# Norm scales applied to the results of the products instead of to the tokens, in a three-block model on one Trainium2 core

## The chip, the core and the metric

The kernel runs on one core of one Trainium2 chip. The core has TensorE (PE, matrix products; its weight loads are shown as PEld), VectorE (DVE), ScalarE (ACT), GpSimd (POOL), and SyncE (SP), which only issues DMAs here. The metric is the device time of one execution in microseconds (us); lower is better. A profile is one execution recorded by the hardware profiler, and its times are counted from its first instruction.

## The reference, cut to what matters

1024 tokens of width 1024 go through three blocks, each with RMS norms in front of its large products. All is float32.

```python
def rmsnorm(x, g):
    xf = x.astype(jnp.float32)
    y = xf * lax.rsqrt(jnp.mean(xf * xf, axis=-1, keepdims=True) + NORM_EPS)
    return (y * g.astype(jnp.float32)).astype(x.dtype)
# block 1
h = rmsnorm(x, norm_g[l]);  proj = h @ w_in[l]                # 1024 -> 4608, split into nine parts
kv = rmsnorm(mem, mem_norm_g[l]) @ w_mem_kv[l]                # 256 memory rows -> 1024
# mLSTM, differential attention, attention on the memory, gates silu(z)
x = rmsnorm(x + concat(y_m, y_d, y_c) @ w_out[l], final_g)
# block 2
proj = rmsnorm_2(h, norm_mix[l]) @ w_in[l]                    # attention, spatial gating, gates
h = h + merged @ w_out[l]
g, up = jnp.split(rmsnorm_2(h, norm_ffn[l]) @ w_ffn_in[l], 2, axis=-1)
h = rmsnorm_2(h + (jax.nn.silu(g) * up) @ w_ffn_out[l], norm_final)
# block 3
proj = rmsnorm_3(h, norm_mix_g[l]) @ w_in[l]                  # recurrent unit, gated convolution
h = h + y @ w_out[l]
m = rmsnorm_3(h, norm_mlp_g[l]) @ w_mlp_up[l]
h = h + jnp.square(jax.nn.relu(m)) @ w_mlp_down[l]
out = rmsnorm_3(h, norm_final_g)
```

At the two joints between blocks two norms are chained: the final norm of a block, whose result is also the next block's residual, and the first norm of the next block.

## The kernel before

**Layout.** Tokens lie transposed: a page `u[k]` has 128 features on the partitions and 1024 tokens along the row, and `h` = 0, 1 picks the half of 512 tokens. A scale per token is therefore a value per column, which must be spread over all partitions.

**Products.** A float32 product is made as three products of a high and a low part (`mm3`, L149 to L151). `split` (L158, L159) makes the parts: ScalarE rounds the source to the high part, VectorE subtracts it for the low part. Weights come in units of 512 KB over SP's queue and are split at L76 and L77. `gemm_fm` runs units of 8 x 3 products of 128x512 into one of two PSUM banks (`ps_mm`, two buffers), then calls `evict`, which reads the bank; TensorE can start unit n+2 only when the bank of unit n is read. With `lag` the first units run all their first halves before any second half.

**The order of the work.** The program is written as generators: a main one that issues product units, and side ones (`spawn`) that advance by one step at each `tick`, about one per unit. A scheduler then puts every engine's instructions in an order by priority (evictions have a raised one); on the chip each engine works its own list in order, so an instruction that waits holds up all behind it.

**A seam** (`seam`, then `norm_gen`, L405). The last output product of a stage (`gemm_out`, first half and then second half of the tokens) adds its results to the pages `u` (L692, L1252, L1646). ScalarE squares each result (L186, L189), GpSimd adds the squares up (L190; at a joint twice, since each of the two chained norms has its own sum). When a half is complete, TensorE sums over the partitions (L198), VectorE takes the inverse root in about a dozen small operations (L174 to L179, L420 to L423), TensorE spreads it over the partitions (L210), ScalarE copies it to SBUF (L433). Only then does VectorE multiply each page by gain and scale (L436), and `split` makes the parts that the next products read. The next `gemm_fm` waits for them.

**The start.** Memory and tokens are loaded; the memory's squares are summed (L186 to L190), its scale is made (L198, L565, L174 to L179, L210, L569), it is scaled (L574) and split, and only then do the eight units on the memory run (four in `gemm_fm`, four in `gemm_tm`). The tokens of each half are squared and added on ScalarE and VectorE (L549, L551), and pass `norm_gen`.

**Other places that are touched.** `block_gemm` (L311) makes two by two blocks of products with seven instead of eight multiplications: GpSimd forms sums of weights (L330 to L335), `operand` splits them, and `out` gets the four result blocks C11, C12, C21, C22 of each pair (L1313 to L1319 in block 2: a silu of C11 and C12; L1667, L1679, L1680 in block 3: a squared relu). `block_tokens` makes the token operands of it and overwrites `u`; `block_up` starts it when the norm generators are done. `residual` (L447) reloads a block's residual and multiplies it by the final norm's gain and scale (L457), the scale being read from DRAM. `down_loads` (L394) reloads hidden values. Evictions of `gemm_fm` write to SBUF with ScalarE's copy or activation, or with both engines.

Of the kernel before, what the change touches and what calls it, by code (L numbers as in the profile page):

```python
# [23 lines left out]
LEAD = dict(norm_g=1, norm_mix_2=3, norm_ffn_2=3, norm_mix_g_3=3, norm_mlp_g_3=3)  # L24
LEAD_F = 2
# [3 lines left out]
LAG = 3  # L29
# [66 lines left out]
class Kern:  # L96
# [56 lines left out]
    def split(self, dst, off, n, src, scale=None):  # L153

        nc = self.nc
        hi, lo = dst[:, 0, off:off + n], dst[:, 1, off:off + n]
        if scale is None:
            nc.scalar.copy(hi, src)  # L158
            nc.vector.tensor_sub(lo, src, hi.bitcast(F32))  # L159
        else:  # L160
            nc.scalar.activation(hi, src, AF.Copy, scale=scale)
            nc.vector.scalar_tensor_tensor(lo, src, scale, hi.bitcast(F32), op0=OP.mult, op1=OP.subtract)
# [50 lines left out]
    def gemm_fm(self, n_units, src, evict, halves=(0, 1), N=512, lag=1, gate=None, post=None, wait=None, ahead=True):  # L213
# [5 lines left out]
        for i, (u, h) in enumerate(order):  # L219
# [7 lines left out]
            for k in range(8):  # L227
# [177 lines left out]
    def norm_gen(self, h, u, g, xs, acc, acc2=None, fg=None, r_d=None, lead=1, stay=False):  # L405

        nc = self.nc  # L410
        n2 = 8 if fg is not None else 4
        for _ in range(lead):
            yield
        ps = self.tp()
        self.sums_to_cols(ps, 0, acc, 4)
        if fg is not None:
            self.sums_to_cols(ps, 4, acc2, 4)
        v = self.nsm.tile([128, 8], F32, name="nv")
        r = self.nsm.tile([128, 8], F32, name="nr")
        nc.vector.tensor_scalar(v[:, :4], ps[:, :4], 1.0 / 1024, EPS, op0=OP.mult, op1=OP.add)  # L420
        if fg is not None:
            nc.vector.tensor_scalar(v[:, 4:], ps[:, 4:8], 1.0 / 1024, None, op0=OP.mult)
            nc.vector.scalar_tensor_tensor(v[:, 4:], v[:, :4], EPS, v[:, 4:], op0=OP.mult, op1=OP.add)  # L423
        self.rsqrt(r[:, :n2], v[:, :n2], n2)
        if fg is not None:
            gg = self.nsm.tile([128, 8], F32, name="ngg")
            nc.vector.tensor_mul(gg, fg, g)
        else:
            gg = g
        yield  # L430
        bps = self.bcast_cols(r[:, n2 - 4:], 4)
        b1 = self.page((128, 2, 512), F32, "rbc")
        nc.scalar.copy(b1[:, 0, :], bps)  # L433
        for k in range(8):
            t = u(k, h) if stay else self.half_tmp("nt")
            nc.vector.scalar_tensor_tensor(t, u(k, h), gg[:, k:k + 1], b1[:, 0, :], op0=OP.mult, op1=OP.mult)  # L436
            x = self.split_page()
            xs[k, h] = x
            self.split(x, 0, 512, t)
            if k % 2:  # L440
                yield
        if fg is not None:
            bps = self.bcast_cols(r, 4)
            nc.scalar.copy(b1[:, 1, :], bps)
            nc.sync.dma_start(r_d[:, h * 512:h * 512 + 512], b1[:, 1, :])
            yield

    def residual(self, u, d, fg, page, name):

        nc = self.nc  # L450
        r = self.page(name="rres")
        nc.gpsimd.dma_start(r, d[8])
        for k in range(8):
            t = page(name=name)
            nc.gpsimd.dma_start(t, d[k])
            yield
            nc.vector.scalar_tensor_tensor(t, t, fg[:, k:k + 1], r, op0=OP.mult, op1=OP.mult)  # L457
            u.append(t)
# [62 lines left out]
    def block1(self):  # L521
# [11 lines left out]
        for i in range(2):  # L533
            (nc.sync if i else nc.scalar).dma_start(memx[i], A["memT"][i])
# [3 lines left out]
        for h in (0, 1):  # L538
            for k in range(8):
# [1188 lines left out]
    def final_gen(self, o, n, u3, acc):  # L1728
        nc, v = self.nc, self.v
        if o + n < 1024:  # L1730
            for _ in range(LEAD_F):
                yield
# [400 lines left out]
```

## Time and profile before

| | us |
|---|---|
| time, median of 3 runs | 3388.26 (3388.24 to 3388.63) |
| time of the profiled execution | 3385.71 |
| span of the profile, first to last instruction | 3383.9 |
| TensorE busy in the span | 3266.0 (97%) |
| VectorE, ScalarE, GpSimd busy | 1937.2, 1169.3, 510.2 |
| mean granted TensorE clock | 0.987 of full speed |

The span is the profiled execution without 1.8 us around it. A busy time counts the instructions' own durations; matrix products overlap, so a busy TensorE is not one at its peak. The granted clock is the share of full speed that the chip allowed TensorE; at the start of the trace, before 30.9 us, none is recorded and the views show 1.00 there.

### The profile page before, as it was taken

To read this page: it belongs to the slowest core of one execution; us is meant where nothing else is said; L and a number is where in the kernel's file an instruction comes from. 1 tells how busy PE (TensorE), PEld (TensorE's weight loads), DVE (VectorE), ACT (ScalarE), POOL (GpSimd) and SP (SyncE) were. 2 spreads that over 40 slices of the span, in tenths; PEclk is the share of its full clock that TensorE was granted. 3 is DMA by queue.
4 is the path that set the end of the run, shared out by engine and by line. 5 is a ranking of instruction groups with operands and counts; after the bars stand their busy time and mean duration, and the time that the engine had idled before them with its cause. 6 is when DMAs were issued, how large, how long until landed. Compare 5 with 4: busy or idle time off the path is not lost. (4 is left out here: it accounts for less than half of the span.)

```text
span 3383.9 us, 41750 instructions
## 1 busy us (share of the span) xinstructions
PE 3266.0 (97%) x16039; PEld 2666.3 (79%) x16039; DVE 1937.2 (57%) x3619; ACT 1169.3 (35%) x2115; POOL 510.2 (15%) x461
## 2 busy tenths in 40 slices
PE   6999999999999999999999999999999989999998
PEld 6788877677777888887788877878878778878887
DVE  7465566664755562446755566455569765554444
ACT  5222344433444442213433342134443433332211
POOL 0000000002200000102423220040211243220002
PEclk9999999999999999999999999999999999999999
DMA  5133211322211244422122244121112233362211
GB/s 188 58 103 127 87 57 38 113 69 78 72 46 42 70 147 159 143 94 103 66 84 85 81 179 148 57 97 54 46 51 75 103 103 109 112 251 94 69 50 56
DMA packets 128632, 318.52 MB, mean 94 GB/s; under 512 B 16305, under 2 KB 34865, under 8 KB 128433
## 3 DMA queue, kind: packets, MB, share of 16 engines
q1 hardware_dynamic: 104976, 236.63, 20.5%
q0 software_dynamic: 21440, 76.51, 6.4%
q8 instruction: 126, 2.06, 0.3%
q10 hardware_dynamic: 2016, 2.72, 0.2%
q14 instruction: 74, 0.60, 0.1%
HBM read 232.90 MB, written 82.90 MB: 93 GB/s over the span
## 5 line engine op out<-in xcount | busy, mean ns | idle before, releaser
L149 PE MATMUL mm<-sp,wsplit 128*128 128x512 f32 (+1 forms) x2880 | 1151.0, 400 | 30.0 <-ACT sp L158 9.7
L150 PE MATMUL mm<-sp,wsplit 128*128 128x512 f32 (+1 forms) x2880 | 1132.4, 393 | 9.5 <-DVE sp L159 7.1
L151 PE MATMUL mm<-sp,wsplit 128*128 128x512 f32 (+1 forms) x2880 | 1129.7, 392 | 0.0
L149 PEld LDWEIGHTS mm<-sp,wsplit 128*128 128x128 f32 x2880 | 547.1, 190 | 149.2 <-ACT sp L158 14.1
L150 PEld LDWEIGHTS mm<-sp,wsplit 128*128 128x128 f32 x2880 | 548.5, 190 | 117.3 <-DVE sp L159 10.2
L151 PEld LDWEIGHTS mm<-sp,wsplit 128*128 128x128 f32 x2880 | 547.7, 190 | 111.4 <-issue 0.4
L358 PE MATMUL mm<-sp,wsplit 128*128 128x512 f32 x1632 | 390.5, 391 | 6.6 <-ACT scp L362 5.0
L76 ACT CAST wsplit<-wraw 128x1024 fp32r<-128x1024 f32 x196 | 205.7, 1049 | 494.3 <-PE mm L151 468.3
L358 PEld LDWEIGHTS mm<-sp,wsplit 128*128 128x128 f32 x1632 | 306.5, 188 | 73.5 <-ACT scp L362 5.4
L77 DVE TENSOR_TENSOR wsplit<-wraw,wsplit 128x1024 fp32r<-128x1024 f32 x196 | 244.8, 1250 | 152.7 <-ACT wsplit L76 145.1
L358 PE MATMUL sc<-sp,wsplit 128*128 128x512 f32 x1224 | 296.6, 391 | 1.3 <-DVE c L372 1.3
L358 PEld LDWEIGHTS sc<-sp,wsplit 128*128 128x128 f32 x1224 | 231.1, 189 | 51.0 <-DVE c L372 1.7
L190 POOL TENSOR_TENSOR acc<-acc,sqt 128x512 f32<-128x512 f32 (+1 forms) x105 | 140.1, 1346 | 474.9 <-ACT sqt L189 388.3
L1646 DVE TENSOR_TENSOR ur<-ur,mm 128x512 f32<-128x512 f32 x112 | 76.8, 686 | 152.1 <-PE mm L151 152.1
L159 DVE TENSOR_TENSOR wsplit<-ssum,wsplit 128x512 fp32r<-128x512 f32 x136 | 101.8, 750 | 89.1 <-ACT wsplit L158 88.9
L1252 DVE SCALAR_TENSOR_TENSOR ur<-mm,ur 128x512 f32<-128x512 f32 x96 | 66.2, 689 | 106.5 <-PE mm L151 106.3
L158 ACT CAST wsplit<-ssum 128x512 fp32r<-128x512 f32 x136 | 82.9, 621 | 109.8 <-POOL ssum L335 36.0
L158 ACT CAST sp<-hraw 128x512 fp32r<-128x512 f32 x108 | 64.0, 620 | 65.2 <-PE mm L151 44.1
L333 POOL TENSOR_TENSOR ssum<-ssum,wraw 128x512 f32<-128x512 f32 x34 | 51.9, 1527 | 221.7 <-DVE wsplit L159 221.7
L158 ACT CAST wsplit<-wraw 128x512 fp32r<-128x512 f32 x102 | 61.8, 620 | 67.4 <-PE sc L358 47.8
L159 DVE TENSOR_TENSOR sp<-hraw,sp 128x512 fp32r<-128x512 f32 x108 | 71.3, 686 | 11.6 <-ACT sp L158 11.6
L335 POOL TENSOR_TENSOR ssum<-wraw,ssum 128x512 f32<-128x512 f32 x34 | 47.3, 1390 | 196.9 <-DVE wsplit L159 196.9
(550 smaller groups left out, 4234.2 us busy)
## 6 DMA issues: line engine op xcount, KB each, us to landing
wraw<-W SPq DMA_DIRECT2D x264, 512.0 KB, 3.7
hraw<-hid_d POOLq DMA_DIRECT2D x54, 512.0 KB, 6.0
hid_d<-scp SPq DMA_DIRECT2D x68, 256.0 KB, 2.0
t_d<-gl SPq DMA_DIRECT2D x32, 256.0 KB, 2.0
u<-x_d POOLq DMA_DIRECT2D x16, 512.0 KB, 6.0
gl<-t_d POOLq DMA_DIRECT2D x32, 256.0 KB, 3.1
u_d<-u SPq DMA_DIRECT2D x32, 256.0 KB, 2.0
ur<-u_d POOLq DMA_DIRECT2D x16, 512.0 KB, 8.2
```

The lines of the kernel that those rows point to most:

```text
L76: K.nc.scalar.copy(s[:, 0, :], r)
L77: K.nc.vector.tensor_sub(s[:, 1, :], r, s[:, 0, :].bitcast(F32))
L149: t.matmul(ps, wh, xh, start=first, stop=False)
L150: t.matmul(ps, wh, xl, start=False, stop=False)
L151: t.matmul(ps, wl, xh, start=False, stop=last)
L158: nc.scalar.copy(hi, src)
L159: nc.vector.tensor_sub(lo, src, hi.bitcast(F32))
L190: eng.tensor_add(acc, acc, t[:, :acc.shape[-1]])
L333: nc.gpsimd.tensor_sub(s, s, a11)
L358: nc.tensor.matmul(d, wk[:, c, :], xk[:, e, :], start=new and k == y == 0, stop=k == 3 and y == 2, skip_group_check=not new)
L1252: nc.vector.scalar_tensor_tensor(uu(m, h), ps, 0.5, uu(m, h), op0=OP.mult, op1=OP.add)
L1646: nc.vector.tensor_add(uu(m, h), uu(m, h), ps)
```

## The change

Each norm is taken apart. Its gain g is a value per feature and stays on the tokens, inside the split. Its scale r is a value per token and is left out of the products; each eviction multiplies the result by r (`row(h)`, r spread over the partitions, or `rc`, r as a column). At a joint the scale of the second norm comes from one sum of squares, weighted with w = sqrt(fg^2 + eps). `feed` scales by g and splits one tile per tick behind the seam's output product; `scale_gen` makes r beside it. `residual` of block 2 makes its own scale from the reloaded pages, and block 3's comes from `row_gen`, which takes the squares of whole pages. `LAG` is 4 instead of 3. One page less is in each of two pools, and the memory and the tokens are loaded in smaller pieces. In the code below "..." marks what is left out.

```diff
@@ gemm_fm
+            while h not in (self.scales if scaled is None else scaled):
+                yield
             with self.tc.high_priority(offset=PRIO_E):
                 evict(u, h, ps)
@@ norm_gen is replaced by
+    def scale_gen(self, h, acc, eps=EPS):
         nc = self.nc
+        for _ in range(LEAD):
             yield
         ps = self.tp()
         self.sums_to_cols(ps, 0, acc, 4)
+        v = self.nsm.tile([128, 8], F32, name="nv")
+        nc.vector.tensor_scalar(v[:, :4], ps[:, :4], 1.0 / 1024, eps, op0=OP.mult, op1=OP.add)
+        r = self.rc[:, 4 * h:4 * h + 4]
+        self.rsqrt(r, v[:, :4], 4)
+        yield
+        yield
+        bps = self.bcast_cols(r, 4)
+        nc.scalar.copy(self.row(h), bps)
+        self.scales.add(h)
+    def feed(self, u, g, xs, done, stay):
+        for h in (0, 1):
+            for k in range(8):
+                while (k, h) not in done:
+                    yield
+                yield
+                t, x = u(k, h), self.split_page()
+                if stay:
+                    self.nc.scalar.activation(t, t, AF.Copy, scale=g[:, k:k + 1])
+                    self.split(x, 0, 512, t)
+                else:
+                    self.split(x, 0, 512, t, g[:, k:k + 1])
+                xs[k, h] = x
+    def row_gen(self, u, d):
+        acc, sq = self.page(name="racc"), self.page(name="rsq")
+        for k in range(8):
+            nc.scalar.activation(sq if k else acc, u[k], AF.Square)
+            if k:
+                nc.gpsimd.tensor_add(acc, acc, sq)
+            yield
+            yield
+        ps = self.tp()
+        self.sums_to_cols(ps, 0, acc, 8)
...
@@ residual
+        for k in range(8):
+            u.append(page(name=name))
+            nc.gpsimd.dma_start(u[k], d[k])
+            yield
+        if not scaled:
+            yield from self.row_gen(u, None)
+            r = self.rrow
+        for k in range(8):
+            nc.vector.scalar_tensor_tensor(u[k], u[k], fg[:, k:k + 1], r, op0=OP.mult, op1=OP.mult)
@@ block1, tokens and memory
             for k in range(8):
+                x = self.split_page()
+                self.split(x, 0, 512, uu(k, h), v("norm_g", k))
+                self.square_sum(acc, uu(k, h), k == 0, eng=nc.gpsimd)
+                xs[k, h] = x
...
+            if k % 2 == 0:
+                s = slice(k % 4, k % 4 + 2)
+                nc.gpsimd.tensor_mul(msq[k // 4][:, s], memx[k // 4][:, s], memx[k // 4][:, s])
+            last = self.split(mview(k), 0, 256, memx[k // 4][:, k % 4, :], v("mem_norm_g", k))
+            if k == 3:
+                with self.tc.issue_after(last[0].ins), self.tc.issue_after(last[1].ins):
+                    self.W.split_to(1)
...
+        def mem_scale():
+            ps = self.tp()
+            for j in (0, 1):
+                for k in range(8):
+                    nc.tensor.matmul(ps[:, j:j + 1], msq[k // 4][:, k % 4, j * 128:j * 128 + 128], self.ones[:, 0:1],
+                                     start=k == 0, stop=k == 7)
@@ evictions: ev_xm, ev_z, ev_qc, ev_d, ev_u, ev_gate and block 3's ev, of this kind
-            nc.scalar.copy(self.xm[u][:, h * 512:h * 512 + 512], ps)
+            nc.vector.tensor_mul(self.xm[u][:, h * 512:h * 512 + 512], ps, self.row(h))
...
-                t = self.half_tmp("zt")
-                self.silu2(t, ps)
+                x, t = self.half_tmp("zx"), self.half_tmp("zt")
+                nc.vector.tensor_mul(x, ps, self.row(h))
+                self.silu2(t, x)
@@ seam
-            self.square_sum(acc[:, s], uu(m, h), m == 0, eng=nc.gpsimd)
-            if fg is not None:
-                self.square_sum(acc2[:, s], uu(m, h), m == 0, v(fg, m), eng=nc.gpsimd)
+            self.square_sum(acc[:, s], uu(m, h), m == 0, 1.0 if w is None else w[:, m:m + 1], eng=nc.gpsimd)
+            done.add((m, h))
             if m == 7:
...
+                gens.append(self.spawn(self.scale_gen(h, acc[:, s], eps)))
@@ block2, out
             if block in ("C11", "C12"):
-                z = self.half_tmp("silu")
+                z, r = self.half_tmp("silu"), self.row(int(block[2]) - 1)
+                nc.vector.tensor_mul(t, t, r)
                 nc.scalar.activation(z, t, AF.Tanh, scale=0.5)
                 nc.vector.scalar_tensor_tensor(t, z, 1.0, t, op0=OP.add, op1=OP.mult)
+                nc.vector.tensor_mul(t, t, r)
@@ block_up
-            while any(g in self.sides for g in gens):
+            while gens[0] in self.sides:
                 yield
@@ block3
+        gens.append(self.spawn(self.row_gen(u2, self.x2_d[8])))
...
-        self.px = px.enter_context(tc.tile_pool(name="px4", side="right", bufs=11))
+        self.px = px.enter_context(tc.tile_pool(name="px4", side="right", bufs=10))
...
         def relu2(m, h, t, x):
-            nc.vector.scalar_tensor_tensor(t, x, 0.0, x, op0=OP.max, op1=OP.mult)
+            nc.vector.scalar_tensor_tensor(t, x, 0.0, self.row(h), op0=OP.max, op1=OP.mult)
+            nc.scalar.activation(t, t, AF.Square)
             store(m, h, t)
```

## Rows read from the trace of the kernel before

**Rows 1.** The page, part 1: busy time, share of the span, instructions.
```profile
PE 3266.0 (97%) x16039; PEld 2666.3 (79%) x16039; DVE 1937.2 (57%) x3619; ACT 1169.3 (35%) x2115; POOL 510.2 (15%) x461
```

**Rows 2.** Windows: stretch, length, busy PE, PEld, DVE, ACT, POOL; clock, DMA share, GB/s.
```profile
0.00:26.20 26.20, 3.19 (x15) 3.05 (x15) 14.91 (x56) 11.51 (x23) 2.77 (x10) 1.00 0.78 292
26.20:60.00 33.80, 29.84 (x207) 27.98 (x208) 30.52 (x60) 22.43 (x40) 4.35 (x8) 1.00 0.52 176
...
840.00:885.00 45.00, 38.37 (x179) 30.81 (x178) 35.18 (x59) 20.88 (x32) 24.22 (x16) 0.96 0.31 101
1565.00:1600.00 35.00, 30.84 (x139) 24.32 (x137) 30.25 (x52) 12.69 (x20) 11.84 (x8) 0.95 0.33 113
1600.00:1650.00 50.00, 46.78 (x197) 37.45 (x196) 46.93 (x59) 23.41 (x42) 21.52 (x13) 0.97 0.15 50
2245.00:2290.00 45.00, 38.45 (x180) 31.22 (x179) 33.55 (x52) 21.54 (x33) 26.26 (x18) 0.96 0.32 106
2635.00:2700.00 65.00, 56.62 (x239) 44.11 (x238) 49.77 (x86) 26.76 (x40) 21.32 (x14) 0.92 0.27 98
2700.00:2760.00 60.00, 50.29 (x199) 40.14 (x199) 47.09 (x56) 23.94 (x44) 34.76 (x20) 0.91 0.24 84
```

**Rows 3.** Waits of PE, whole span: who waited for whom; us, times, longest.
```profile
PE tp L198 <- DVE macc L190: 15.8, 1, 15.8
PE mm L149 <- ACT sp L158: 9.7, 5, 3.1
...
PE mm L150 <- DVE sp L159: 7.1, 4, 3.0
PE tp L210 <- DVE memr L179: 5.9, 1, 5.9
```

**Rows 4.** Timeline, second seam: start, us, engine, line, [idle before it, releaser].
```profile
1589.98 0.73 PE L149 MATMUL mm<-sp,wsplit 128*128 128x512 f32 x2 [3.11 <-ACT sp L158]
...
1587.53 2.41 DVE L436 SCALAR_TENSOR_TENSOR u<-u,vec,rbc 128x512 f32<-128x512 f32 x2
```

**Rows 5.** Windows just behind that wait, columns as in Rows 2.
```profile
1590.80:1594.20 3.40, 3.40 (x9) 2.25 (x8) 2.56 (x3) 0.00 (x0) 1.38 (x1) 0.50 0.47 155
```

**Rows 6.** Timeline of the start, ACT and PE.
```profile
5.26 1.05 ACT L76 CAST wsplit<-wraw 128x1024 fp32r<-128x1024 f32 x1 [2.25 <-DMA wraw<-W]
...
23.17 1.71 PE L198 MATMUL tp<-ones,acc 128*128 128x1 f32 x8
```

**Rows 7.** Tile memx: its two DMAs.
```profile
L534 SPq DMA_DIRECT2D memx<-memT x1: 422/422/422, 1.2 to 1.2; - x1
...
DMA to landing us min/median/max: 6.3/6.7/7.1
```

**Rows 8.** Tile ms: durations ns, first and last start; last, PE's idle time.
```profile
L149 PE MATMUL mm<-ms,wsplit x32: 278/283/582, 26.2 to 40.4; 128*128 128x256 f32 x32
...
L151 PE MATMUL mm<-wsplit,ms x32: 278/283/283, 41.0 to 57.2; 128*128 128x256 f32 x32
L158 ACT CAST ms<-mt x8: 398/404/406, 25.7 to 30.2; 128x256 fp32r<-128x256 f32 x8
...
  DVE wsplit L77: 5.8, 4
```

**Rows 9.** Lines L436 and L692: durations min/median/max ns.
```profile
L436 DVE SCALAR_TENSOR_TENSOR u<-u,vec,rbc x32: 733/745/1784, 1572.4 to 2704.9; 128x512 f32<-128x512 f32 x32
...
L692 DVE TENSOR_TENSOR u<-u,mm x48: 673/687/690, 686.8 to 867.9; 128x512 f32<-128x512 f32 x48
```

**Rows 10.** Windows of two longer stages, columns as in Rows 2.
```profile
600.00:840.00 240.00, 229.58 (x1132) 174.35 (x1132) 142.60 (x292) 84.68 (x167) 26.57 (x33) 0.95 0.26 89
...
1650.00:2000.00 350.00, 350.00 (x1546) 289.82 (x1545) 182.44 (x258) 125.29 (x223) 107.38 (x80) 1.00 0.25 83
```

**Rows 11.** DVE's groups, 1650 to 2000: busy us, mean ns, idle before, releaser.
```profile
L1314 DVE SCALAR_TENSOR_TENSOR c<-silu,c 128x512 f32<-128x512 f32 x19 | 22.8, 1202 | 0.8 <-ACT silu L1313 0.8
```

**Rows 12.** POOL's groups over the whole span, columns as in Rows 11.
```profile
L1784 POOL TENSOR_TENSOR wsplit<-cmask,ctaph 128x1024 fp32r<-128x1024 f32 x18 | 48.8, 2718 | 142.8 <-PE mm L1558 89.2 <-PE mm L151 40.3 <-PE mm L1802 10.5
```

More of the change, by code (lines that the diff above doesn't have):

```diff
@@ L402, in down_loads, with new_scales, row @@
             m += n
-    def norm_gen(self, h, u, g, xs, acc, acc2=None, fg=None, r_d=None, lead=1, stay=False):
+    def new_scales(self, paged=False):
+        self.rb = self.page((128, 2, 512), name="rb") if paged else self.rbp.tile([128, 2, 512], F32, name="rb", tag="rb")
+        self.rc = self.nsm.tile([128, 8], F32, name="rc")
+        self.scales = set()
+    def row(self, h):
+        return self.rb[:, h, :]
+    def scale_gen(self, h, acc, eps=EPS):
         nc = self.nc
-        n2 = 8 if fg is not None else 4
-        for _ in range(lead):
+        for _ in range(LEAD):
             yield
@@ L433, in norm_gen @@
-        nc.scalar.copy(b1[:, 0, :], bps)
-        for k in range(8):
[L435 to L439, printed above, removed]
+        nc.vector.tensor_scalar(v, ps[:, :8], 1.0 / 1024, EPS, op0=OP.mult, op1=OP.add)
+        self.rsqrt(r, v, 8)
+        yield
+        yield
+        for h in (0, 1):
+            bps = self.bcast_cols(r[:, 4 * h:4 * h + 4], 4)
+            nc.scalar.copy(sq[:, h * 512:h * 512 + 512], bps)
@@ new lines, in row_gen, with residual @@
+        if d is not None:
+            nc.sync.dma_start(d, sq)
+        self.rrow = sq
+    def residual(self, u, d, fg, page, name, scaled):
+        nc = self.nc
+        r = None
+        if scaled:
+            r = self.page(name="rres")
+            nc.gpsimd.dma_start(r, d[8])
+        for k in range(8):
+            u.append(page(name=name))
+            nc.gpsimd.dma_start(u[k], d[k])
+            yield
+        if not scaled:
[3 more added lines that the diff above has]
+            nc.vector.scalar_tensor_tensor(u[k], u[k], fg[:, k:k + 1], r, op0=OP.mult, op1=OP.mult)
@@ L440, in norm_gen @@
             if k % 2:
                 yield
[L442 to L458, printed above, removed]
@@ new lines, in block1 @@
+        with self.tc.issue_after(last[0].ins), self.tc.issue_after(last[1].ins):
+            self.W.split_to(2)
+        r = self.small([128, 2], F32, "memr", 1)
+        rb = self.half_tmp("mrb")
+        def mem_scale():
[4 more added lines that the diff above has]
+                                     start=k == 0, stop=k == 7)
+            vv = self.small([128, 2], F32, "memv", 1)
+            nc.vector.tensor_scalar(vv, ps[:, :2], 1.0 / 1024, EPS, op0=OP.mult, op1=OP.add)
+            self.rsqrt(r, vv, 2)
+            bps = self.bcast_cols(r, 2)
+            nc.scalar.copy(rb[:, :256], bps[:, :256])
@@ L725, in seam @@
         xs = {}
-        acc, acc2 = self.page(name="acc"), None
+        acc = self.page(name="acc")
+        gg, w, eps = v(g), None, EPS
         if fg is not None:
-            acc2 = self.page(name="acc2")
+            gg, w, t = (self.nsm.tile([128, 8], F32, name=n) for n in ("ngg", "nw", "nwt"))
+            nc.vector.tensor_mul(gg, v(fg), v(g))
+            nc.vector.tensor_mul(t, v(fg), v(fg))
+            nc.vector.tensor_scalar(t, t, EPS, None, op0=OP.add)
+            self.rsqrt(w, t, 8)
+            nc.vector.tensor_mul(w, w, t)
+            eps = EPS * EPS
         uu = lambda k, h: u[k][:, h * 512:h * 512 + 512]
-        gens = []
+        self.new_scales(g == "norm_mix_g_3")
+        done = set()
+        gens = [self.spawn(self.feed(uu, gg, xs, done, stay))]
         def ev(m, h, ps):
@@ L1730, in final_gen @@
         if o + n < 1024:
-            for _ in range(LEAD_F):
+            for _ in range(LEAD):
                 yield
```

178 lines of the change are left out of this document (85 added, 93 removed).

## The prediction

> **What bounds the kernel now.** I read the page first: TensorE is busy for 3266.0 of 3383.9 us [rows 1]. The change removes no product, so all that it can win is TensorE's idle time, 117.9 us, and the time that the clock then runs low: a mean of 0.987 over the span is 44 us of full speed. Next the windows, to find where these 162 us lie. The start holds 23.0 us of idle time before 26.2 us and 4.0 behind it; five stretches at the four seams (the last two at the MLP of block 3) hold the rest that the change aims at [rows 2]. A stretch loses its length less PE's busy time, plus the missing share of the clock times its length: 840 to 885 loses 6.6 + 1.8 = 8.4; 1565 to 1600 4.2 + 1.7 = 5.9; 1600 to 1650 3.2 + 1.5 = 4.7; 2245 to 2290 6.5 + 1.8 = 8.3; 2635 to 2700 8.4 + 5.2 = 13.6; 2700 to 2760 9.7 + 5.4 = 15.1. Together 56 us. Then the waits, for what PE waits for there: at the start the sum of the memory's squares (15.8) and its inverse root (5.9), at the seams the high and low parts of tokens that have just been scaled (9.7 and 7.1) [rows 3]. The timeline of one seam shows why: a product stands 3.11 us for a high part whose source VectorE is just scaling, two operations of together 2.41 us [rows 4]. Behind that wait the granted clock is 0.50, that is 1.2 instead of 2.4 GHz, for 3.4 us, which costs 1.7 us more [rows 5]. So a short wait here costs about half as much again.
>
> **The start.** Now the first product on the memory starts at 26.2 and the last one at 57.2 [rows 8]. The change splits the loaded memory at once. The first weights are there at 5.26 [rows 6]; the memory's two DMAs leave at 1.2 and land 6.3 to 7.1 us later, at 7.5 to 8.3 [rows 7], and in four pieces the first should be earlier. Four splits of 0.40 [rows 8] and one weight split of 1.05 [rows 6] on ScalarE then put the first product at about 10, 16 us earlier. Some of it is given back. The sums over the partitions are now one per page and token block, 16 instead of 2, so 32 instructions instead of 4; eight took 1.71 us [rows 6], so 28 more cost 6.0 at that pace and about half at the higher clock level: 4.5. The first unit's eviction must wait for the memory's scale. Two units fill the two banks; the chain of the inverse root kept PE waiting 5.9 us [rows 3], and one unit in between covers 31 us / 8 = 3.9 of it [rows 8], so 2 to 3 us remain. The slow clock of the first products is the same in both kernels. 16 - 4.5 - 2.5 = **9 us earlier**, with 4 to 14 as bounds: the low end because VectorE, busy 30.5 of 33.8 us there [rows 2], already held these products up for 5.8 us with weight splits [rows 8], the high end if the sums and the chain hide.
>
> **The seams.** `feed` splits a tile one tick after its residual is added, so the tokens of a half are ready when its last product ends, and the scale is wanted only by an eviction. For the second half that is the fifth unit, with `LAG` 4, four units of 24 products behind the seam. What stays: VectorE still adds, splits weights and tokens, and overwrites `u` for the block products, all against GpSimd, and 2635 to 2700 also holds waits of the convolution's own norm. Of the 56 us I take two thirds, **38 us**, with 24 and 48 as bounds. At the two joints one sum of squares and one spreading fall away and `row_gen` brings as much back at another place; that is nothing on TensorE.
>
> **What the evictions add.** An extra VectorE operation from PSUM costs 0.69 us [rows 9]; by the code there are about 164 of these, some 40 of them in place of a copy by ScalarE, and 84 more from SBUF. About 80 scalings of 0.745 us or more (L436) go [rows 9]. VectorE gains some 60 to 100 us of work on 1937 and is not the bound [rows 1]. It costs where TensorE already waits for small chains. From 600 to 840 TensorE loses 10.4 us and 5% of the clock, 22 us in all [rows 10]; with the other attention and mLSTM stages about 31 us. One more operation of 0.69 per unit is some 13% more for VectorE; I take 5 us, between 0 (the banks are read at least as early as now) and 12.
>
> **Block products of block 2.** Each of 20 pairs gets four multiplications by `row(h)` with both inputs in SBUF. VectorE now needs 182.4 of 350 us [rows 10], 18.5 pairs, so 9.9 us per pair of 18.9. The trace shows what such an operation costs beside GpSimd: the same scaling takes 0.733 alone and up to 1.784, while one that reads PSUM stays at 0.690 at most, though GpSimd works there too [rows 9]; the silu from SBUF here takes 1.20 in the mean [rows 11]. The Trainium skill, page "SBUF — State Buffer", section "Who interferes with whom", says that a VectorE instruction with two SBUF inputs contends with a GpSimd one that reads SBUF, and one with a single SBUF input does not; the trace agrees (1.784 against 0.690), and by that rule these multiplications would be the dear ones. Four times 0.69 to 1.78 is 2.8 to 7.1 us, 12.7 to 17.0 of 18.9 per pair. It fits. I put 2 us, of 0 to 40.
>
> **Smaller terms.** `row_gen` adds whole pages on GpSimd; the nearest row of that size is 2.72 us [rows 12]. In block 2 seven of them (19 us) stand in GpSimd's list among the loads of the gates, which the evictions need every other unit: 2.5 us, of 0 to 8. In block 3 they run beside the recurrent unit: 1, of 0 to 4. The page pools of the block products lose one page each; the eleventh page of block 3 (the first copy of C11) then waits for a weight page: 2, of 0 to 6. ScalarE gets 64 squares and some scalings; at 35% [rows 1] they hide, and without that cover would cost 0.6 each.
>
> **Sum.** 9 + 38 - 5 - 2 - 2.5 - 1 - 2 = 34.5. The profiled execution took 3385.7, which gives 3351.2; the median of the runs is 2.6 above it, so **3353.5 us**.
>
> **Rivals.**
> 1. *The waits at the seams only change their name.* The splits stay on VectorE, at up to 1.78 us beside GpSimd's additions [rows 9], and `feed` goes one tile per tick, so the last tiles of a half can still be late. For it: in 1565 to 1650 VectorE is busy 77.2 of 85 us [rows 2]. Against: a scaling per tile leaves VectorE just there. Only 15 of the 56 come back: 3353.5 + 23 = 3376.5. Chance 0.17.
> 2. *The start does not move,* since weight splits on VectorE set its pace [rows 2, 8]: 3353.5 + 9 = 3362. Chance 0.12.
> 3. *VectorE becomes the bound in the block products of block 2.* An addition that clears a bank has one group of 12 products as its cover before P4 needs that bank. If the new multiplications, by the upper price above, stand ahead of it, TensorE waits in every pair and its clock drops as at the seam [rows 4, 5]: 2 us + 1.7 us, 20 times, is 74 instead of 2: 3425. It makes the kernel slower than before from 1.8 us lost per pair. Against: that stage now loses nothing at all, and half of VectorE's time is free [rows 10]. Chance 0.06.
> 4. *Everything hides.* The seams give 48, the start 14, and the added work costs 3: 3327. For it: evictions clear a bank with one operation instead of two. Chance 0.15.
> 5. *The change does not do what it says:* scales come so late that evictions fill both banks at each seam. Now the chain runs within a half of the output product, eight units of 12 products; it would need twice that. 3385 to 3390, that is no change. Chance 0.05.
>
> The forecast itself has 0.45: 3340 to 3367 by its inner bounds.
>
> **How the numbers follow.** About 0.2%, 6.8 us, is what a measurement of this kernel tells from no change. Faster than 3381.5: the forecast, 4 and 2, and nearly all of 1: 0.87. Within: case 5 and the edge of 1: 0.07. Slower: case 3: 0.06. The range reaches from case 4 to the far side of case 1: 3325 to 3381.
>
> **What would show it.** In the profile after: the first large product near 10 us and the last on the memory near 48; no wait of PE for `sp` at L149 and L150 behind the seams, and a granted clock near 1.00 there; L198 and L210 no longer among PE's waits apart from the start. PE's idle time should fall from 117.9 to some 85 us. The forecast is wrong if 1650 to 2000 is no longer full, if PE waits for evictions in the attention stages, or if the seam windows keep their losses.

## The result, and the profile after

The changed kernel takes **3426.66 us** (median of 4 runs, 3424.2 to 3429.4); the kernel before takes 3388.25 in runs beside it. The ratio is **1.0116, 95% interval 1.0099 to 1.0134**: 38 us slower. The forecast was 3353.5, with 3325 to 3381 as its range: the wrong side, by 73 us. TensorE is idle for 137.1 of 3424.6 us, where [rows 1] leave 117.9 and the forecast about 85. The first row is the page's busy line of after; then come the waits of PE over the span (who waited for whom: us, times, longest), two such rows of the kernel before, and windows of after (columns as in [rows 2]) at the start, in the attention on the memory, at block 2's residual, at the second seam and at the MLP's seam.

```profile
PE 3287.5 (96%) x16067; PEld 2688.0 (78%) x16067; DVE 2084.8 (61%) x3805; ACT 1205.2 (35%) x2141; POOL 521.4 (15%) x464
```

```profile
PE tp L207 <- DVE rc L176: 21.2, 8, 7.4
PE tp L195 <- POOL acc L187: 13.2, 4, 5.7
PE tp L616 <- POOL msq L602: 8.1, 3, 7.4
PE tp L207 <- DVE brr L176: 6.0, 2, 3.6
PE mm L148 <- ACT wsplit L75: 5.9, 1, 5.9
...
PE tp L195 <- POOL racc L453: 4.4, 1, 4.4
PE mm L1885 <- DVE wsplit L1867: 4.3, 2, 3.6
...
PE sc L148 <- ACT mp L833: 3.7, 4, 0.9
PE mm L148 <- DVE g3x L1694: 3.6, 1, 3.6
...
PE mm L148 <- ACT sp L157: 2.3, 1, 2.3
```

```profile
PE tp L210 <- DVE nr L179: 8.0, 7, 2.5
...
PE tp L198 <- POOL acc L190: 3.8, 2, 1.9
```

```profile
15.40:58.00 42.60, 30.09 (x204) 28.45 (x204) 34.92 (x56) 23.68 (x39) 16.54 (x15) 0.88 0.53 183
440.00:490.00 50.00, 42.13 (x202) 32.52 (x202) 29.87 (x85) 19.28 (x55) 0.51 (x1) 0.83 0.19 62
1450.00:1500.00 50.00, 38.30 (x150) 30.61 (x149) 34.60 (x40) 12.15 (x15) 20.34 (x14) 0.86 0.19 64
1600.00:1650.00 50.00, 41.03 (x167) 32.67 (x167) 43.50 (x68) 26.17 (x43) 25.33 (x16) 0.90 0.26 91
...
2685.00:2745.00 60.00, 49.78 (x214) 39.38 (x213) 52.09 (x73) 38.09 (x59) 33.55 (x21) 0.91 0.28 98
```

L195 makes the column sums (L198 before), L207 spreads the inverse root (L210 before). Of the waits for split tokens that [rows 3] show, 9.7 and 7.1 us, only 2.3 us are left. In their place TensorE, which follows its list, stands longer at its own smallest instructions: 21.2 us for the inverse root from VectorE (8.0 before), of which 1.8 at the start, and 13.2 for GpSimd's additions (3.8 before), of which 1.9 at the final norm.

**Where the time goes.** Both kernels run the same 13,792 large products (128x512 and 128x256), so the n-th of them can be compared: its start in one trace less its start in the trace before. (The order differs for some 360 of them, nearly all between 117 and 1105 us.) The table is worked out from these starts. A row is a stretch between two products (second column: when it runs in the kernel before), a number is the us that a kernel loses in it (+) or wins (-) against the kernel before; the names of the experiments follow below.

```
stretch                 before, us  after lam_early qt_own sums_beh start_dve row_spr resid_seam later seam_dve before_dve combo combo_later conv_dve
start                      0- 117   +6.4   +4.5   +7.6   +3.1   -0.4   +8.1   +7.5  +10.5   +6.9   +1.5   -3.3   +0.7   -2.6
mLSTM                    117- 445   +0.8   +1.4   +0.1   +0.8   +1.2   +0.8   +0.8   +0.8   +0.7   +0.1   +0.0   +0.3   +0.0
attention on the memory  445- 506  +15.7   +6.4   +0.8  +16.8  +18.3  +15.7  +18.3  +17.1  +18.3   +0.1   +0.8   +0.8   +0.8
diff. attention          506- 649   +1.1   +0.1   +0.6   +0.3   +2.5   +1.2   +1.9   +1.0   +1.7   +1.4   +0.4   +0.6   +0.4
first seam               649-1105  -10.8   -5.1   -7.9  -11.6   -5.1  -11.6   -8.5  -11.3  -15.8   -5.2  -13.2  -10.5   -6.7
block 2, gates          1105-1418   +0.9   +1.6   +1.5   +1.6   +0.8   +1.6   +3.7   +1.3   +0.7   +0.8   +4.4   +4.0   +4.2
block 2, residual       1418-1523  +21.9  +21.9  +21.4  +22.0  +22.6  +12.4   +0.0  +21.9  +23.2   +0.0   +0.0   -0.0   +0.0
second seam             1523-1674   +3.7   +3.8   +3.9   +3.7   +3.8   +3.2   +3.4   -1.3   -1.8   -5.8   -0.6   -5.2   -0.4
block products, down    1674-2249   +4.4   +4.2   +5.6   +4.5   +6.3   +4.1   +4.6   +6.4   +4.4   -1.1   -0.0   +4.5   +3.4
third seam              2249-2331   -2.2   -2.2   -3.3   -2.2   -1.1   -2.2   -2.2   +2.2   -8.7   -4.2   -8.7   -4.5   -8.7
block 3, convolution    2331-2630   +8.4   +9.6   +8.8   +6.6   +9.6   +9.3   +6.5   +8.4   +8.5   +0.4   +8.1   +8.3   -6.3
MLP's seam to the end   2630-3372   -9.8  -11.3   -8.2  -11.7   -9.7  -11.1  -10.9  -17.0  -23.5   -9.8  -24.1  -18.5  -22.9
sum                               +40.6  +35.0  +31.0  +33.9  +48.8  +31.4  +25.1  +39.9  +14.8  -21.9  -36.1  -19.4  -38.6
```

Each column is one profiled execution. A stretch that an edit leaves alone mostly repeats to 1 to 3 us, the start between +4.5 and +8.1. The row of the first seam varies from -5 to -12 without any edit there, but the variation lies in the attention ahead of the seam (649 to 823 us); the seam itself (823 to 912) repeats at -8.8 to -9.7, is at -14.6 in seam_dve and at -6.5 in before_dve. Four places make the loss: the residual of block 2, the attention on the memory, the convolution, the start. The rows of the seams win 19 us of the 38 forecast.

### The profile page after: what moved, and what is told of

Same layout as the page of the kernel before. It is cut to its first block, busy times and chain, and to the rows that moved or that the text cites. A ratio compares the mean times of both kernels' runs of the same rounds, so it can differ in the third digit from the quotient of the medians.

```text
span 3424.6 us, 42133 instructions
## 1 busy us (share of the span) xinstructions
PE 3287.5 (96%) x16067; PEld 2688.0 (78%) x16067; DVE 2084.8 (61%) x3805; ACT 1205.2 (35%) x2141; POOL 521.4 (15%) x464
## 3 DMA queue, kind: packets, MB, share of 16 engines
q10 hardware_dynamic: 2160, 2.72, 0.2%
## 4 chain that ended last, share of the span: by engine, by line
PE 81%; DVE 10%; issue 3%; ACT 3%; DMA 2%; POOL 1%; ACTq 0%; POOLq 0%; DVEq 0%; SPq 0%
PE mm L148 17%; PE mm L149 17%; PE mm L150 17%; PE mm L357 10%; PE sc L357 8%; PE mm L1885 1%; DVE sp L157 1%; PE tp L149 1%; PE tp L148 1%; PE sc L1139 1%; DVE wsplit L76 1%; PE sc L1463 1%; DMA hraw<-hid_d 1%; DVE sp L159 1%; PE tp L150 1%
## 5 line engine op out<-in xcount | busy, mean ns | idle before, releaser
L187 POOL TENSOR_TENSOR acc<-acc,sqt 128x512 f32<-128x512 f32 (+1 forms) x91 | 121.3, 1333 | 526.5 <-ACT sqt L186 433.0
L1733 DVE TENSOR_TENSOR ur<-ur,mm 128x512 f32<-128x512 f32 x112 | 76.9, 686 | 147.4 <-PE mm L150 147.4
L157 DVE TENSOR_TENSOR wsplit<-wraw,wsplit 128x512 fp32r<-128x512 f32 x102 | 68.8, 687 | 14.5 <-ACT wsplit L157 14.1
```

What stands on the lines that cost most here:

```text
L157: return nc.scalar.copy(hi, src), nc.vector.tensor_sub(lo, src, hi.bitcast(F32))
L187: eng.tensor_add(acc, acc, t[:, :acc.shape[-1]])
L1733: nc.vector.tensor_add(uu(m, h), uu(m, h), ps)
```

## Experiments

All start from the changed kernel, except the one named before_dve.

### Attention on the memory: what holds the next stage's evictions?

The lanes of the attention on the memory are long chains of small products; in the kernel before, products of the next stage fill the time between them. In the changed kernel those run out at 451.8 us and come back at 476.3. Meanwhile TensorE runs the lanes alone, with waits under 1 us at each step, and the clock falls (0.83 in 440 to 490, above). VectorE's timeline (start, us, engine, line) has the first eviction of the next stage, L732, only here:

```profile
473.94 0.20 DVE L1098 TENSOR_TENSOR lamt<-lamr 1x64 f32<-1x64 f32 x1
...
475.46 0.20 DVE L1101 TENSOR_REDUCE lams<-lamt 1x1 f32<-1x64 f32 x1
475.59 0.67 DVE L732 TENSOR_TENSOR qt<-mm,rb 128x512 f32<-128x512 f32 x1
```

Two edits put more into the ring of four half tiles: the scaled results (`qt`), and `lamr` and `lamt` of `lam_setup`, which had tiles of their own.

```diff
# lam_early: moved from behind the lanes
         qc = {}
+        self.lam_setup()
# qt_own: two tiles of its own for ev_qc and ev_d
+        qp = es.enter_context(self.tc.tile_pool(name="qp", bufs=2))
-            t = self.half_tmp("qt")
+            t = qp.tile([128, 512], F32, name="qt", tag="qt")
```

> The small vector that weights the differential attention (lam_setup) is made before the attention on the memory instead of behind it; nothing else is moved. Between the 1740th and the 1800th large product the changed kernel loses 13.8 us against the kernel before, with the first eviction of the next stage (L732) at 475.6 us, right behind lam_setup's operations on VectorE. Theory A: lam_setup's two tiles, which the change put into the ring of four half tiles, stand between the memory lanes and those evictions; then some 12 us come back, 3426.7 - 12 = 3415. Theory B: the evictions' own new half tiles wait for the lanes' half tiles in the same ring, lam_setup only passes by; then under 4 us come back, 3423 to 3427.

Measured: 3418.66 us, 8.0 less than the changed kernel and between the two theories; in the stretch 9.3 of the 15.7 us come back.

> The evictions of the queries on the memory and of the queries and keys of the differential attention write their scaled results to two tiles of their own instead of the shared ring of four half tiles; a pool of eight pages gives one page for that. Theory B (the evictions wait for the lanes' tiles in the ring): some 13 us come back, 3414. Theory A (lam_setup stands in the way, on VectorE's list): under 4 us, 3423 to 3427. A page less in the pool could cost some 2 us in either case.

Measured: 3416.94 us. In the stretch 14.9 of 15.7 come back; the whole run gains only 9.7, since other stretches of this run (the first seam's row above all) lie some us higher than in the column after. The window 440 to 490 is full, at full clock, though the small vector is still made in the old place:

```profile
440.00:490.00 50.00, 49.92 (x272) 38.96 (x272) 34.58 (x99) 22.13 (x62) 0.51 (x1) 1.00 0.14 50
```

The two theories do not exclude each other: the ring is the cause in both. An eviction may not write before the tile four places back is released, and by the code that one belongs to a lane (`zl`, L853) that is still running. Taking the vector out shortens the queue; taking the evictions out ends it.

### The residual of block 2

`row_gen` squares a page on ScalarE and adds it on GpSimd, alternating over one page. This is the line of the additions in both blocks (minimum, median, maximum in ns) and who waited for it, then two of them in POOL's timeline, then PE's waits in the stretch.

```profile
L453 POOL TENSOR_TENSOR racc<-racc,rsq x14: 2329/2394/2408, 1450.8 to 2345.1; 128x1024 f32<-128x1024 f32 x14
...
  ACT rsq L451: 28.1, 12
```

```profile
1450.79 2.40 POOL L453 TENSOR_TENSOR racc<-racc,rsq 128x1024 f32<-128x1024 f32 x1
1454.36 2.39 POOL L453 TENSOR_TENSOR racc<-racc,rsq 128x1024 f32<-128x1024 f32 x1 [1.17 <-ACT rsq L451]
```

```profile
1461.46 0.64 PE L148 MATMUL mm<-sp,wsplit 128*128 128x512 f32 x1 [3.48 <-DVE gl L1342]
...
1474.99 3.29 PE L195 MATMUL tp<-ones,racc 128*128 128x1 f32 x16 [4.44 <-POOL racc L453]
...
1488.91 0.76 PE L148 MATMUL mm<-sp,wsplit 128*128 128x512 f32 x1 [3.67 <-DVE u L1330]
```

Three waits of 11.6 us, with the clock at 0.86 in 1450 to 1500: first a gate's eviction, which waits beside GpSimd's additions, then the column sums, then an eviction that stands behind the eight scalings.

```diff
# row_spread: all loads in one step, one step per square instead of two
             for k in range(8):
                 u.append(page(name=name))
                 nc.gpsimd.dma_start(u[k], d[k])
-                yield
+            yield
# resid_seam: the sum of squares of the residual's norm again at the first seam
+            if acc2 is not None:
+                self.square_sum(acc2[:, s], uu(m, h), m == 0, eng=nc.gpsimd)
...
+            nc.sync.dma_start(r_d[:, h * 512:h * 512 + 512], t)
```

> In block 2 the residual's own scale is made from pages that are all loaded in one step, with one step for each page's square instead of two: 12 steps instead of 28, while the loop that runs beside it has 16. The changed kernel loses 22 us there (1450 to 1527 us) against the kernel before. Theory: the chain is not through when the products that cover it end, and its column sums, inverse root and eight scalings then stand bare; some 18 us come back, 3409. Rival: GpSimd's seven additions of whole pages, or the loads, set its end however it is spread: under 6 us, 3421 or more.

Measured: 3418.54 us, 8.1 less; in the stretch 9.5 of 21.9 come back, between the two. The column sums no longer wait, but the gates' evictions do, at three places instead of one (3.48, 1.67 and 1.44 us).

> Undoes one part of the change: the final norm of block 1 has its own sum of squares again at the seam, its scale goes to DRAM there, and the residual of block 2 reads it back, with no row of its own. Theory: the 22 us that the residual costs at 1450 to 1527 come back, and the seam of block 1 pays up to 4 us for a second square and addition per tile: 3426.7 - 18 = 3409, some 8 us better than spreading the row thinner. Rival: the place loses its time by the eight scalings on VectorE and the loads, which stay: under 8 us, 3419 or more.

Measured: 3409.94 us, 16.7 less, as expected. The stretch is at +0.0, the stretch of the gates pays some 3 us. The place of the row and GpSimd's whole-page additions cost the 22 us; the eight scalings, which stay, cost nothing.

### The start

TensorE's first 32 instructions are the sums of the memory's squares. VectorE then stands for their result, and the first weight's low part stands behind that on VectorE's list (timeline):

```profile
15.58 0.16 DVE L619 TENSOR_SCALAR memv<-tp 128x2 f32<-128x2 f32 x1 [4.24 <-PE tp L616]
...
16.25 1.23 DVE L76 TENSOR_TENSOR wsplit<-wraw,wsplit 128x1024 fp32r<-128x1024 f32 x1
```

```diff
# sums_behind
+                with self.tc.issue_after(self.last_mm.ins):
+                    mem_scale()
# start_dve: the same, and
-                self.square_sum(acc, uu(k, h), k == 0, eng=nc.gpsimd)
+                self.square_sum(acc, uu(k, h), k == 0)
```

> The 32 small products that sum the memory's squares, and the chain of the inverse root behind them, are put behind the last product of the first memory unit in the lists; before that they are TensorE's first instructions, which wait for GpSimd's squares until 15.6 us while VectorE stands 4.2 us for their result. Theory: this order costs the start; the first large product comes at about 12 instead of 15.4, and some 5 us are left of it at 117 us: 3426.7 - 5 = 3422. Rival: splits of weights and tokens on VectorE and ScalarE set the pace of the start, the gain is given back before 60 us: within 2 us of 3427.

Measured: 3421.93 us. The first product comes at 10.3, so the order was the cause of the late beginning. But the last memory product still ends at 57.7: the lead of 16 us is used up there, as the rival says, and of the whole start 3.3 us remain, about what the start varies by without an edit. Where the lead goes is in PE's timeline, first of after, then of sums_behind:

```profile
35.10 0.58 PE L148 MATMUL mm<-ms,wsplit 128*128 128x256 f32 x1 [5.89 <-ACT wsplit L75]
```

```profile
40.23 1.87 PE L195 MATMUL tp<-ones,acc 128*128 128x1 f32 x8 [6.42 <-POOL acc L187]
```

In the changed kernel a product stands for a weight's high part, which stands behind the tokens' squares and splits on ScalarE's list; in sums_behind TensorE stands at the tokens' column sums for GpSimd's additions. Both kernels begin the first unit on tokens about when the kernel before does (0.5 and 0.6 us later). The rest of the changed kernel's 6.4 us is lost in the units behind it, where the granted clock is 0.88 between 58 and 100 us, 1.00 in the kernel before.

> The memory's sums stand behind the first unit as in sums_behind, and VectorE instead of GpSimd adds up the squares of the tokens at the start. In sums_behind the first product came at 10.3 but the last memory product still ended at 57.8: ScalarE split no weights between 24.4 and 39.4 us. Theory: its squares wait in the ring of half tiles for GpSimd's additions, and the weight splits stand behind them; without GpSimd the last memory product ends near 52 and the start is some 6 us better than in sums_behind: 3416. Rival: VectorE, which gets 14 more operations of 0.7 us, is the pace: no better than sums_behind, 3421 to 3427.

Measured: 3424.87 us (3413.97 to 3434.53), too wide for a verdict on 3 us. In the stretch itself the start is 3.5 us better than with sums_behind (-0.4 against +3.1). In combo, conv_dve and combo_later, which hold the same two edits, the start is at -3.3, -2.6 and +0.7, so a gain over the changed kernel is there. The reason given was wrong in its path: in sums_behind ScalarE waits only 1.0 us for GpSimd's sums between 20 and 60. It is TensorE that waits for them, the 6.42 us above, and with VectorE's additions 1.75.

### The seams: place in the list, or slow additions?

At the MLP's seam seven additions run back to back on GpSimd, and the column sums wait for the last of them (timeline of POOL and of PE):

```profile
2695.42 12.20 POOL L187 TENSOR_TENSOR acc<-acc,sqt 128x512 f32<-128x512 f32 x7 [86.13 <-ACT acc L183]
```

```profile
2707.67 1.87 PE L195 MATMUL tp<-ones,acc 128*128 128x1 f32 x8 [5.71 <-POOL acc L187]
```

The first of two edits moves the small instructions back. `LEAD` is the number of steps ahead of the column sums; the kernel before has three at the seams, the changed kernel two. The second edit gives the additions to VectorE.

```diff
# later
-LEAD = 2
+LEAD = 4
...
         self.rsqrt(r, v[:, :4], 4)
-        yield
-        yield
+        for _ in range(4):
+            yield
# seam_dve
-            self.square_sum(acc[:, s], uu(m, h), m == 0, 1.0 if w is None else w[:, m:m + 1], eng=nc.gpsimd)
+            self.square_sum(acc[:, s], uu(m, h), m == 0, 1.0 if w is None else w[:, m:m + 1])
```

> scale_gen waits four steps instead of two before the column sums, and four instead of two between the inverse root and its spreading; the final norm keeps its two. In the changed kernel TensorE stands 13.2 us at column sums (L195) and 21.2 us at spreadings (L207), all of one kind: small instructions that stand in its list ahead of products that are ready. Theory 1: they only stand too early; both waits fall under 10 us together and, with the clock, some 25 us come back: 3402. Rival: the chain itself is late, since GpSimd's additions and VectorE's splits slow each other; the wait moves to the evictions, under 6 us come back: 3421 or more.

Measured: 3422.35 us, 4.3 less: the rival. No wait of over 1 us is left at L195 behind a seam, but L207 still waits up to 6.8 us, and evictions (L1733) 1.8 and 2.0. The second seam and the MLP's win 12 us, the third seam and the start lose 8.5.

> At the four seams the squares are added up by VectorE instead of GpSimd; all else is as in the changed kernel. There GpSimd's additions take 1.3 to 2.2 us, seven in a row when the residual additions come in a bunch, and VectorE's splits beside them 1.0 to 1.8 instead of 0.7. Theory 2: this mutual slowing makes the sums late; the column sums no longer wait (13.2 us before), VectorE's splits go back to 0.7, and some 15 us come back: 3412. Rival (list order alone, or VectorE too full with 14 more operations of 0.7 us per half): under 5 us, 3422 or more.

Measured: **3396.04 us**, 30.6 less, twice what was expected. The second, third and MLP's seam win 5.5, 6.5 and 13.7 us. PE's waits for `acc` at column sums fall from 13.2 to 1.9 us, which is the final norm's, where GpSimd still adds; those at spreadings fall from 21.2 to 15.0. The groups of DVE and POOL at the MLP's seam, first of after (2685 to 2745), then of seam_dve (2665 to 2720): count, busy us, mean ns.

```profile
L187 POOL TENSOR_TENSOR acc<-acc,sqt 128x512 f32<-128x512 f32 x14 | 22.4, 1597 | 101.5 <-ACT acc L183 86.1 <-ACT sqt L186 14.9
L157 DVE TENSOR_TENSOR sp<-u,sp 128x512 fp32r<-128x512 f32 x17 | 19.6, 1173 | 3.0 <-ACT sp L157 3.0
...
L1733 DVE TENSOR_TENSOR u<-u,mm 128x512 f32<-128x512 f32 x12 | 8.1, 678 | 1.9 <-PE mm L150 1.9
```

```profile
L157 DVE TENSOR_TENSOR sp<-u,sp 128x512 fp32r<-128x512 f32 x17 | 12.3, 739 | 0.0
...
L1733 DVE TENSOR_TENSOR u<-u,mm 128x512 f32<-128x512 f32 x15 | 10.2, 682 | 1.2 <-PE mm L150 1.0
L187 DVE TENSOR_TENSOR acc<-acc,sqt 128x512 f32<-128x512 f32 x14 | 9.6, 684 | 1.4 <-ACT acc L183 0.9 <-ACT sqt L186 0.4
```

An addition takes 0.684 instead of 1.597 us, a split 0.739 instead of 1.173. The 17 splits and 14 additions need 21.9 us of VectorE, where the splits alone needed 19.6. The seam's window and the page's busy line of seam_dve say the same:

```profile
2665.00:2720.00 55.00, 52.65 (x241) 41.62 (x240) 49.47 (x94) 42.71 (x66) 1.37 (x1) 1.00 0.38 133
```

```profile
PE 3283.8 (97%) x16067; PEld 2690.0 (79%) x16067; DVE 2081.3 (61%) x3861; ACT 1206.7 (36%) x2141; POOL 440.7 (13%) x408
```

VectorE runs 56 instructions more and is busy 3.5 us less; GpSimd is rid of 80.7 us. Over the whole changed kernel 28 of these splits run beside an addition or product of GpSimd and take 1.17 us in the mean; 36 run without one and take 0.68. Which half of it counts more, the shorter sum or the faster splits, was not separated.

### Is it the change that makes the seams depend on this?

```diff
# before_dve: the kernel before, with
-            self.square_sum(acc[:, s], uu(m, h), m == 0, eng=nc.gpsimd)
+            self.square_sum(acc[:, s], uu(m, h), m == 0)
# and the same for acc2
```

> The kernel before with one edit: VectorE instead of GpSimd adds up the squares at its seams. If the mutual slowing of the two engines costs every seam, the kernel before gains too, some 5 to 12 us: 3377 to 3385. If it is the change that made the seams depend on it (the sums are wanted while the splits still run, on lists that TensorE follows), the kernel before gains nothing, or loses up to 15 us since its VectorE also has the scalings there (77 of 85 us busy): 3390 to 3405.

Measured: **3362.43 us**, ratio to the kernel before 0.9924 (0.991 to 0.9938). The kernel before gains 24.5 us, twice the upper end of what was expected: GpSimd's additions held up its seams as well. They explain 30 us of the changed kernel's time, but not that it is slower than the kernel before. With the additions on VectorE in both it is still slower by 0.9% (1.0018 against 0.9924 of the kernel before, 32 us), not much less than 1.2%.

### All together

```diff
# combo = qt_own + resid_seam (second sum on VectorE) + seam_dve + sums_behind + start_dve
# conv_dve = combo, with both halves of the convolution's weights on VectorE:
-            for a, eng in enumerate((self.nc.gpsimd, self.nc.vector)):
+            for a, eng in enumerate((self.nc.vector, self.nc.vector)):
# and the final norm's additions on VectorE; combo_later = combo + later
```

> The changed kernel with the parts that cost it taken back: own tiles for the evicted queries and keys as in qt_own, squares at the seams added by VectorE as in seam_dve, block 1's final scale made at its seam as in resid_seam (its second sum on VectorE too), the memory's sums behind the first unit and the tokens' squares added by VectorE at the start as in start_dve. Theory: the losses lie at separate places and add up. Read from the curves of the single runs: 14.8 + 26 + 19 + 7 = 67 us of 3426.7, so 3360, faster than the kernel before by some 30 us. Rival: VectorE, which gets the work of all of them, takes back half: 3390, about the kernel before.

Measured: **3351.15 us**, ratio 0.9898 (0.988 to 0.9915). The losses add up: 75 us come back, 67 were counted, and the medians of the single runs give 59. Most of this is not the change's merit: before_dve, the kernel before with one edit, stands at 0.9924 (0.991 to 0.9938). What the change is worth beside it is 11 us of 3362, with intervals that touch, and the combination has taken one part of the change back (block 1's own sum of squares).

> The combination with two further moves from GpSimd to VectorE: the high halves of the convolution's weights (L1867 in the changed kernel, 1.9 to 2.9 us on GpSimd, 2.9 instead of 1.2 us on VectorE beside it) and the squares of the final norm. Theory: the mutual slowing also makes the stage of the convolution lose the 8.1 us that the combination still loses there (9300th to 10640th product); 5 of them and 2 at the end come back: 3351 - 7 = 3344. Rival: two halves of 1.2 us on VectorE per 2.85 us of convolution products leave no room for its recurrent unit; the stage loses 5 to 15 us more: 3356 to 3366.

Measured: **3341.13 us**, ratio 0.9861 (0.9845 to 0.9876), the fastest of all, near the first theory. The convolution goes from +8.1 to -6.3; the final norm's additions show no gain in their row (-24.1 and -22.9). The convolution weights' low halves on VectorE, beside GpSimd's high halves, in combo, and then both halves on VectorE in conv_dve (18 instructions each: busy us, mean ns):

```profile
L1886 DVE TENSOR_TENSOR wsplit<-cmask,ctap 128x1024 fp32r<-128x1024 f32 x18 | 30.2, 1694 | 6.8 <-PE mm L1904 2.3 <-issue 2.2 <-PE mm L150 1.6
```

```profile
L1886 DVE TENSOR_TENSOR wsplit<-cmask,ctaph 128x1024 fp32r<-128x1024 f32 x18 | 22.0, 1221 | 2.7 <-PE mm L150 1.4 <-PE mm L1660 0.8 <-PE mm L1904 0.5
L1886 DVE TENSOR_TENSOR wsplit<-cmask,ctap 128x1024 fp32r<-128x1024 f32 x18 | 21.9, 1219 | 0.0
```

One half beside GpSimd cost VectorE 30.2 us, both halves alone 43.9.

> The combination with the later small instructions of the run later (four steps ahead of the column sums, four ahead of the spreading). The combination still stands 5.9, 5.6 and 1.5 us at spreadings behind two seams. Theory: with the sums no longer late, the place in TensorE's list is what remains; those waits vanish and some 10 us with the clock come back: 3341. Rival: the inverse root's small operations are late on VectorE, wherever TensorE asks for them; the wait moves to evictions: 3348 to 3354.

Measured: 3362.91 us, 12 more than combo and more than either theory gave. Later small instructions lose 4.2 us at the third seam, 5.6 at the MLP's and 4.0 at the start, and win 4.6 at the second; the rest lies in stretches that vary. The waits do not vanish: TensorE stands 15.5 us at spreadings for VectorE's inverse root, 13.0 in combo. A later place in the list is not what the seams lacked; why it costs so much was not followed up.

## Why the prediction was wrong, step by step

**The start: forecast 9 us earlier, measured 6.4 later.** The time of the first weights was right: 10.3 in sums_behind. The step that failed is the price of the 28 more column sums: 4.5 us, as if beside or behind the first products. They stand ahead of all of them in TensorE's list and wait for GpSimd's squares, and the first product comes at 15.4. The second failure is "last memory product near 48". With the first product 16 us earlier than before, sums_behind still ends the memory's products at 57.7, and of all runs none began the next unit more than 3.5 us earlier than the kernel before. Rival 2, that the start does not move, had this right, its reason only in part: in the changed kernel it is ScalarE's half of a weight (5.9 us), in sums_behind the tokens' column sums (6.4 us).

**The seams: forecast 38 us, measured 19.1 in their four rows,** and some 12 if these are narrowed to the seams themselves (823 to 912, 1523 to 1674, 2249 to 2331 and 2630 to 2758 us of the kernel before). The reading of [rows 3] was right as far as it went: the splits do not wait for a scaling any more. But the clock is 0.90 and 0.91 at two seams, not 1.00. The step that failed is "the scale is wanted only by an eviction": TensorE's own small instructions make the scale, and they stand in its list ahead of products that are ready. The sum took away the named waits and left their place empty. Rival 1 had the size nearly right (15 us of the 56) by another road: not late splits but late sums. Its price, 1.78 us beside GpSimd, was the clue; with GpSimd out of the way the four rows win some 47 to 50 us (combo, seam_dve), near the top of the bounds. Of these 25 are open to the kernel before as well. At the narrowed seams it is 39 and 43 us, and 27 for before_dve: about half of the 56 us comes back with the scalings left in place. So the step that the seams "hold the rest that the change aims at" failed too; with VectorE's additions in both kernels the change itself wins 12 to 16 us there.

**The evictions: forecast 5 us (0 to 12), measured 26.9** (15.7 at the memory, 8.4 at the convolution, 2.8 elsewhere; block 3's `row_gen` is not in it, its column sums stand at 2365 us and the convolution's row begins at 2373 of the changed kernel). For the extra operations themselves the price holds: the mLSTM, the differential attention and the gates lose 2.8 us together. What was missing is the tile that each of them writes. The step "between 0 (the banks are read at least as early as now)" failed: an eviction that wants a tile of a ring of four reads its bank when the ring allows it, not when VectorE is free. At the convolution conv_dve shows a VectorE that is slowed by GpSimd. That the new evictions are what it was then short for is argued, not shown: the kernel before was not run with that edit.

**Block products of block 2: forecast 2 us, measured 2.3** for these (1674 to 2003 us of the kernel before) and 2.1 for the output products behind them. Rival 3 did not come: two of the four multiplications take 1.18 us in the mean and two 0.69, inside the prices given, and they matter little where half of VectorE's time is free. That its 3425 us meets the measured time is chance.

**`row_gen` in block 2: forecast 2.5 us (0 to 8), measured 21.9.** The row was right, 2.39 us against the 2.72 of [rows 12]. But square and addition alternate over one page, 3.57 us from one addition to the next (1450.79 and 1454.36), so seven take 25 us, and the program gives the row 28 steps where the products beside it have 16. The step that failed is "queued among the loads of the gates": the prediction asked who waits in GpSimd's list, and not when the column sums come up in TensorE's. The page pools (2 us) show no loss of their own in any stretch; the block products of block 3 win 1.8 us. Block 3's `row_gen` (1 us) runs in the row of the third seam and was not separated.

The sum itself ends 0.3 us low: 3351.2 and 2.6 make 3353.8. It changes nothing.

In the prediction the Trainium skill's page "SBUF — State Buffer", section "Who interferes with whom", was weighed for the block products alone. Its rule, that a VectorE instruction with two SBUF inputs contends with a GpSimd one that reads SBUF, bears on every split of the seams. The trace agrees: 1173 ns for the split beside GpSimd and 739 without it, 678 and 682 for the residual addition, which has one input in PSUM. The Trainium skill, page "Perfetto Trace Analysis", section "Optimizing GPSIMD Operations", says: "Prefer implementations on other engines where possible." The runs agree for the additions of the seams: 30.6 and 24.5 us.

## What to carry to other kernels

When an edit removes a wait, list what stands next in the same engine's list, its smallest instructions too, and ask when their inputs come; count the tiles that a new intermediate result takes, not only its operation. Elementwise work with two SBUF inputs that runs on GpSimd "for free" beside VectorE can be dearer than on VectorE itself; try it there before anything is restructured, and give the kernel before the same chance, or its gain is booked to the change.

## What the runs showed of the hardware

That work could be moved to VectorE at no cost in its busy time: 56 additions more, and 2081.3 instead of 2084.8 us.
